# One block of 128 columns for the shared keys and index keys, copied on ScalarE to the rows of their heads

## The chip, the cores and the metric

The kernel runs on one core of one Trainium2 chip. The metric is the device time of the whole program in microseconds (us); a lower time is better. One launch computes everything, and all weights are read from the chip's memory in it.

## The reference, cut to what matters

Two blocks run one after the other on 256 tokens of width 1024: a block of two hybrid attention layers, and a block with a gated delta rule and 16 experts. The change lies in the hybrid layers. Each projects its input with one wide matrix and splits the columns:

```python
h = split_cols(u @ w_in)                     # 4032 columns per layer
dq = rope(h["dsa_q"].reshape(B, S, 4, 64), pos)
dk = rope(h["dsa_k"][:, :, None, :], pos)[:, :, 0]        # 64 columns, one key for 4 heads
iq = rope(h["idx_q"].reshape(B, S, 8, 32), pos)
ik = rope(h["idx_k"][:, :, None, :], pos)[:, :, 0]        # 32 columns, one key for 8 index heads
isc = jnp.einsum("bthd,bsd->bths", iqb, ik)               # scores that choose the top 64 tokens
isc = jnp.einsum("bth,bths->bts", iwb, jax.nn.relu(isc))
...
s = jnp.einsum("bthd,btkd->bthk", qb, kg) * scale         # attention over the chosen tokens
```

The four attention heads share one key of 64 columns, and the eight index heads share one index key of 32.

## The kernel before, in words

Projections are kept transposed: a tile of 128 columns of the projection becomes 128 partitions by 256 tokens. `CHUNKS` lists what is projected in order; most chunks are pairs of such tiles, and one transfer on SyncE's queue brings the 1 MB of weights of a pair into one of two buffers `w`. For each tile `proj_t` calls `halves`, which splits the weights into a rounded part `wh` (a cast on ScalarE, L349) and a remainder `wl` (a subtraction, L350), and then issues 24 matmuls of 128x128 by 256 columns (L438 to L440: eight steps of three).

The heads of a tile stand on different rows (partitions), and a matmul of scores takes query and key from the same rows. So a shared key has to stand on the rows of every head. Before, the columns did that: tile `dk` repeats the 64 key columns twice, and tile `ik` repeats the 32 index key columns four times; both are projected in full. `rope` copies the projected tile to `rraw` on ScalarE (L525), multiplies it by a rotation matrix on TensorE (L531), by the sine on VectorE (L533) and by the cosine on GpSimd (L534), and adds the two on VectorE (L535) into a tile `qk`. `topk` starts when `ik`, `iq0` and `iq1` have been through this.

Which engine subtracts in `halves` is set by a counter over the whole program:

```python
def lo_engine(self):
    self.nsplit += 1
    return self.nc.gpsimd if self.pat[self.nsplit % len(self.pat)] == "P" else self.nc.vector
```

`pat` is "VVP" (every third on GpSimd), except for "P" in chunks 3 to 5 of a layer and a few places of the second block. `act_halves` uses the same counter for activations.

The order of the instructions on each engine is not the order of the code: a scheduler sets it when the program is built, from the dependencies and its own estimate of times, and at run time each engine works through its list in order.

The expert weights (16 experts, 12 transfers of 1 MB each) come through a ring of 21 buffers and the two `w` buffers. They are all issued on SyncE's queue, and a transfer waits until its buffer is free.

Of the kernel before, what the change touches and what calls it, by code (L numbers as in the profile page):

```python
# [34 lines left out]
HALF = slice(0, 64), slice(64, 128)  # L35
# [19 lines left out]
def _cols(name, a, b):  # L55
    return list(range(_OFF[name] + a, _OFF[name] + b))
# [6 lines left out]
    return out  # L63


_TILES = {"dk": _cols("dsa_k", 0, 64) * 2, "ik": _cols("idx_k", 0, 32) * 4}
for _i in range(2):
    _TILES[f"iq{_i}"] = _cols("idx_q", 128 * _i, 128 * _i + 128)
    _TILES[f"dq{_i}"] = _cols("dsa_q", 128 * _i, 128 * _i + 128)
# [8 lines left out]
for _i in range(3):  # L78
# [2 lines left out]
        + _cols("fox_v", 0, 128) + _cols("dsa_v", 0, 32),  # L81
        "NB": _cols("fox_v", 128, 384),
        "NC": _cols("nsa_vs", 0, 128) + _cols("nsa_vw", 0, 128)}
CHUNKS = ["NA", ("dk", "ik"), ("iq0", "iq1"), ("dq0", "dq1"), ("kc", "vc"), ("fq0", "fk0"), "NB",
          ("fq1", "fk1"), ("fq2", "fk2"), "NC", ("ks", "kw"), ("nq0", "nq1"), ("nq2", "g0"), ("g1", "g2"),
          ("g3", "g4"), ("g5", "g6"), ("g7",)]

# [1 line left out]
def _chunk_cols(c):  # L89
    return _NAT[c] if isinstance(c, str) else sum((_TILES[t] for t in c), [])  # L90


WIN_COLS = sum((_chunk_cols(c) for c in CHUNKS), [])
assert sorted(set(WIN_COLS)) == list(range(4032))
WIN_N = len(WIN_COLS)
WIN_OFF = np.cumsum([0] + [len(_chunk_cols(c)) for c in CHUNKS])
MIX_ROWS = list(range(640)) + [640 + 64 * h + i for h in NSA_PERM for i in range(64)]
# [91 lines left out]
def prep(inp):  # L189
# [18 lines left out]
    w = f["w_in"][:, :, WIN_COLS].reshape(2, 8, 128, WIN_N).transpose(0, 2, 1, 3)  # L208
    parts = [w[:, :, :, WIN_OFF[i]:WIN_OFF[i + 1]].reshape(2, 128, -1) for i in range(len(CHUNKS))]
    a["w_in"] = np.concatenate(parts, axis=2)  # L210
# [39 lines left out]
class Kern:  # L250
# [424 lines left out]
    def layer(self, l, uT, x, m, hook, first=None):  # L675

        nc = self.nc
# [3 lines left out]
        S = {}  # L681
        qk = lambda: self.t([128, 256], "qk", 12)
        for i, ch in enumerate(CHUNKS):
            if ch == ("kc", "vc"):
                cc = self.compress_consts(l)
            hook(i)
            self.pat = "P" if 3 <= i < 6 else "VVP"
            w = self.load_chunk(l, i) if l or i else first
            if isinstance(ch, str):
                N = self.t([128, 2, 256], ch)  # L690
                p = self.mmt()
                self.proj_n(p, w, uT)
                nc.vector.tensor_copy(N, p)
                S[ch] = N
                if ch == "NA":
                    self.after_na(N, bf, S)
                continue
            p = self.mmt()
            for ti, name in enumerate(ch):
                q = p[:, ti, :]  # L700
                self.proj_t(q, w[:, :, 128 * ti:128 * ti + 128], uT)
                if name[:2] in ("iq", "ik", "dk", "dq", "ks", "kw"):
                    S[name] = qk()
                    self.rope(S[name], q, 32 if name[0] == "i" else 64)
                elif name in ("kc", "vc"):
                    S[name] = self.compress(cc, 0 if name == "kc" else 1, q)
                elif name[0] == "g":
                    j = int(name[1])
                    e = self.t([128, 256], "ge", 2)
                    self.sigmoid_big(e, q)  # L710
                    nc.vector.tensor_mul(e, e, q)
                    g = S[f"mix{j}"]
                    nc.vector.tensor_mul(g, g, e)
                else:
                    S[name] = qk()
                    nc.scalar.copy(S[name], q)
                    if name[:2] == "nq":
                        S["r" + name] = qk()
                        self.rope_sb(S["r" + name], S[name], 64)
                if name == "iq1":  # L720
                    self.topk(S)
                if name == "dq0":
                    self.dsa(S, 0)
                if name == "dq1":
                    self.dsa(S, 1)
                if name == "vc":
                    self.cmp_finish(cc, S)
                if name[:2] == "fk" and name != "fk1":
                    self.fox(S, int(name[2]))
                if name == "nq2":  # L730
                    self.nsa(S)
            if ch == ("fq1", "fk1"):
                self.fox(S, 1)
# [1252 lines left out]
```

## Time and profile before

| | |
|---|---|
| three runs | 1263.03 us median (1259.28 to 1269.72) |
| profiled execution, own time | 1266.42 us |
| profiled execution, span from first to last instruction | 1264.6 us |
| TensorE busy | 1019.2 us (81% of the span) |
| VectorE / ScalarE / GpSimd busy | 540.9 / 388.1 / 282.4 us |
| data moved | 330 MB, mean 261 GB/s |

The span is 1.8 us shorter than the profiled execution's own time, and that execution was 3.4 us longer than the median. Busy shares are means over stages that differ: the first 820 us hold the two attention layers and the delta rule, the rest the experts.

### The profile page before, as it was taken

Reading aid. Unit: us, or ns where it says so; the run is one execution under the profiler, and the core shown is the slowest. Engines: PE = TensorE matmul, PEld = TensorE weight load, DVE = VectorE, ACT = ScalarE, POOL = GpSimd, SP = SyncE. Lnnn points to the kernel's source line nnn. Section 1 sums busy time; section 2 is a strip of 40 time slices with the busy share of each in tenths; the row PEclk is TensorE's granted clock in tenths of the full one; section 3 lists DMA queues with packets and bytes.
Section 4 is the critical chain, followed back from the end, with each engine's and each line's share of the span. In section 5 each row is a group of like instructions: output and inputs, shape, how many; then the busy total and the mean of one; then the engine's idle time right before and its main releaser. Section 6 shows DMA issues by size and latency. Waiting matters only on the chain. (4 is left out here: it accounts for less than half of the span.)

```text
span 1264.6 us, 22819 instructions
## 1 busy us (share of the span) xinstructions
PE 1019.2 (81%) x9488; PEld 715.0 (57%) x9488; DVE 540.9 (43%) x1269; ACT 388.1 (31%) x905; POOL 282.4 (22%) x253
## 2 busy tenths in 40 slices
PE   5889999978879999948879988897666776676675
PEld 2767777767766777736768777654222332332232
DVE  2585457686687445586585346511000100010002
ACT  2344437636344436535452535210000000000002
POOL 1442132276541231253326352000000000000000
PEclk7899999998799999979989999798888777787678
DMA  9747864334235483621202456799999999999996
GB/s 365 257 161 254 318 236 152 136 128 188 81 105 201 155 316 117 237 98 67 95 24 101 179 231 274 292 382 419 420 421 418 421 418 421 419 420 420 421 419 251
DMA packets 52696, 330.07 MB, mean 261 GB/s; under 512 B 8305, under 2 KB 10097, under 8 KB 14449
## 3 DMA queue, kind: packets, MB, share of 16 engines
q1 hardware_dynamic: 52592, 328.61, 65.9%
q8 instruction: 74, 1.21, 0.4%
q14 instruction: 30, 0.24, 0.0%
HBM read 327.54 MB, written 1.05 MB: 260 GB/s over the span
## 5 line engine op out<-in xcount | busy, mean ns | idle before, releaser
L438 PE MATMUL mm<-uT,wh 128*128 128x256 f32 x576 | 173.3, 301 | 6.4 <-ACT wh L349 3.2
L440 PE MATMUL mm<-uT,wl 128*128 128x256 f32 x576 | 168.4, 293 | 11.2 <-POOL wl L350 9.0
L349 ACT CAST wh<-w 128x1024 fp32r<-128x1024 f32 x124 | 127.9, 1034 | 145.2 <-PE mm L439 81.8
L350 POOL TENSOR_TENSOR wl<-w,wh 128x1024 fp32r<-128x1024 f32 x51 | 123.4, 2423 | 204.5 <-ACT wh L349 186.2
L439 PE MATMUL mm<-uT,wh 128*128 128x256 f32 x576 | 168.5, 293 | 0.0
L440 PEld LDWEIGHTS mm<-uT,wl 128*128 128x128 f32 x576 | 113.1, 197 | 18.0 <-POOL wl L350 10.4
L438 PEld LDWEIGHTS mm<-uT,wh 128*128 128x128 f32 x576 | 113.1, 196 | 17.2 <-issue 7.4
L439 PEld LDWEIGHTS mm<-uT,wh 128*128 128x128 f32 x576 | 113.2, 196 | 6.8 <-issue 6.0
L1847 PE MATMUL o<-rw,XE 128*32 128x256 f32 x944 | 87.4, 475 | 34.7 <-DMA rw<-in_w_gate 34.7
L1847 PE MATMUL g<-rw,XE 128*32 128x256 f32 x928 | 82.7, 462 | 39.4 <-DMA rw<-in_w_up 39.4
L350 DVE TENSOR_TENSOR wl<-w,wh 128x1024 fp32r<-128x1024 f32 x73 | 92.1, 1262 | 51.4 <-ACT wh L349 49.4
L1859 ACT ACTIVATE hd<-o 128x256 f32<-128x256 f32 x16 | 6.1, 384 | 313.0 <-PE o L1847 313.0
L1863 DVE TENSOR_TENSOR hd<-hd,g 128x256 f32<-128x256 f32 x16 | 6.7, 418 | 212.5 <-PE g L1847 212.5
L1891 PE MATMUL mm<-rw,hT 128*32 128x256 f32 x880 | 64.2, 429 | 22.0 <-DMA rw<-in_w_down 16.5
L1847 PEld LDWEIGHTS g<-rw,XE 128*32 128x32 f32 x928 | 31.5, 126 | 84.6 <-DMA rw<-in_w_up 66.0
L1847 PEld LDWEIGHTS o<-rw,XE 128*32 128x32 f32 x944 | 31.8, 129 | 79.5 <-DMA rw<-in_w_gate 54.9
L462 PE MATMUL mm<-wh,uT 128*128 128x256 f32 x256 | 53.8, 298 | 9.7 <-DVE yT L1261 6.6
L1891 PEld LDWEIGHTS mm<-rw,hT 128*32 128x32 f32 x880 | 27.4, 120 | 49.4 <-DMA rw<-in_w_down 22.8
L462 PEld LDWEIGHTS mm<-wh,uT 128*128 128x128 f32 x256 | 41.6, 194 | 15.0 <-ACT wh L349 9.5
L571 ACT ACTIVATE P<-s,nm 128x256 f32<-128x256 f32 (+1 forms) x88 | 35.8, 418 | 28.9 <-DVE nm L564 26.9
L481 PE MATMUL s<-wh,m 128*128 128x512 f32 x128 | 40.9, 396 | 0.0
L462 PE MATMUL mm<-wl,uT 128*128 128x256 f32 x128 | 37.6, 294 | 0.8 <-DVE wl L350 0.7
(645 smaller groups left out, 1941.9 us busy)
## 6 DMA issues: line engine op xcount, KB each, us to landing
rw<-in_w_gate SPq DMA_DIRECT2D x59, 1024.0 KB, 19.9
rw<-in_w_up SPq DMA_DIRECT2D x58, 1024.0 KB, 19.9
rw<-in_w_down SPq DMA_DIRECT2D x55, 1024.0 KB, 19.9
w<-in_w_in SPq DMA_DIRECT2D x48, 1024.0 KB, 4.7
wg<-in_w_mod SPq DMA_DIRECT2D x24, 1024.0 KB, 5.2
wg<-in_w_ada SPq DMA_DIRECT2D x21, 1024.0 KB, 5.5
w<-in_w_out SPq DMA_DIRECT2D x12, 1024.0 KB, 4.8
w<-in_w_up SPq DMA_DIRECT2D x6, 1024.0 KB, 19.8
```

The lines of the kernel that those rows point to most:

```text
L349: self.nc.scalar.copy(hi, w)
L350: self.lo_engine().tensor_sub(lo, w, hi)
L438: mm(out, wh[:, k, :], uh[:, k, :], start=(k == 0), stop=False)
L439: mm(out, wh[:, k, :], ul[:, k, :], start=False, stop=False)
L440: mm(out, wl[:, k, :], uh[:, k, :], start=False, stop=(k == 7))
L462: mm(p[:, tt, :], a[:, k, t], b[:, k % 4, :], start=(k == 0 and tt == 0 and j == 0), stop=(k == 7 and j == 2), skip_group_check=True)
L481: mm(Y(tt, n), a[:, t], b[:, 512 * n:512 * n + 512], start=(k2 == 0 and kk == 0 and i == 0), stop=(k2 == 3 and kk == 1 and i == 2))
L571: nc.scalar.activation(Pm[:, h, o:o + n], S[:, h, o:o + n], AF.Exp, bias=nm[:, i:i + 1], scale=0.125, accum_out=l[:, i:i + 1])
L1847: nc.tensor.matmul(pp[32 * j:32 * j + 32, :], XE[:, k, 32 * (e % 4):32 * (e % 4) + 32], w[:, kk, 256 * j:256 * j + 256], start=(k == 0), s ...
L1859: last = nc.scalar.activation(hd, pg, AF.Silu)
L1863: nc.vector.tensor_mul(hd, hd, pu)
L1891: nc.tensor.matmul(py[32 * j:32 * j + 32, :], hT[:, cb, 32 * jj:32 * jj + 32], w[:, kk, 256 * j:256 * j + 256], start=(k == 0), stop=(k == 7))
```

## The change

`dk` and `ik` become one tile `di` of 128 columns: the 64 key columns and the 32 index key columns twice. It is projected once, as a chunk of its own with 0.5 MB of weights. From the result ScalarE copies rows 0 to 63 to both halves of a tile `rraw` for the keys, and rows 64 to 127 to both halves of another for the index keys. From there `rope_sb` does for each what it did before. The matmuls of scores see the same tiles as before.

```diff
-_TILES = {"dk": _cols("dsa_k", 0, 64) * 2, "ik": _cols("idx_k", 0, 32) * 4}
+_TILES = {"di": _cols("dsa_k", 0, 64) + _cols("idx_k", 0, 32) * 2}
...
-CHUNKS = ["NA", ("dk", "ik"), ("iq0", "iq1"), ("dq0", "dq1"), ("kc", "vc"), ("fq0", "fk0"), "NB",
+CHUNKS = ["NA", ("di",), ("iq0", "iq1"), ("dq0", "dq1"), ("kc", "vc"), ("fq0", "fk0"), "NB",
...
-                if name[:2] in ("iq", "ik", "dk", "dq", "ks", "kw"):
+                if name == "di":
+                    for n, rows, d in (("dk", HALF[0], 64), ("ik", HALF[1], 32)):
+                        raw = self.t([128, 256], "rraw", 2)
+                        for to in HALF:
+                            nc.scalar.copy(raw[to], q[rows])
+                        S[n] = qk()
+                        self.rope_sb(S[n], raw, d)
+                elif name[:2] in ("iq", "dq", "ks", "kw"):
                     S[name] = qk()
                     self.rope(S[name], q, 32 if name[0] == "i" else 64)
```

Per layer there is one call of `halves` less, so the counter of `lo_engine` stands one lower for everything behind it in layer 0, and two lower from layer 1's chunk 2 on. The scheduler builds a new order from this. It shows at three places of layer 0, right behind chunk `NA`. (Lines behind 702 are numbered 8 higher in the changed kernel.)

ScalarE, before: the casts of `dk` and `ik`, then one copy to `rraw` ahead of the cast for `iq0`.

```order
L782 ACTIVATE lfe<-lfe 128x12
L349 CAST wh<-w 128x1024
L783 ACTIVATE lfe<-lfe 128x12
L349 CAST wh<-w 128x1024
L797 CAST foxc<-g 96x256
L663 ACTIVATE c2s<-c2s 128x16
L525 COPY rraw<-mm 128x256
```

ScalarE, changed: the cast of `di` first, and the casts of the next four tiles behind the four copies of `di`.

```order
L349 CAST wh<-w 128x1024
L789 ACTIVATE lfe<-lfx 128x12
L663 ACTIVATE ng<-ng 128x36
L790 ACTIVATE lfe<-lfe 128x12
L791 ACTIVATE lfe<-lfe 128x12
L805 CAST foxc<-g 96x256
L707 COPY rraw<-mm 64x256 x4
L663 ACTIVATE c2s<-c2s 128x16
L349 CAST wh<-w 128x1024 x4
```

What moved: the first cast stands ahead of the activations of `lfe`, and nothing but copies stands between the projection of `di` and the cast that `iq0` needs.

GpSimd, before: the subtraction for `iq0` alone, and two more behind the cosine product of `ik`.

```order
L816 TENSOR_SCALAR foxl<-foxc,c_263 96x256 x2
L534 TENSOR_TENSOR qk<-rraw,c_263 128x256
L816 TENSOR_SCALAR foxl<-foxc,c_263 96x256
L350 TENSOR_TENSOR wl<-w,wh 128x1024
L534 TENSOR_TENSOR qk<-rraw,c_263 128x256
L350 TENSOR_TENSOR wl<-w,wh 128x1024 x2
```

GpSimd, changed: both cosine products of `di`, then three subtractions in a row.

```order
L534 TENSOR_TENSOR qk<-rraw,c_263 128x256
L824 TENSOR_SCALAR foxl<-foxc,c_263 96x256
L534 TENSOR_TENSOR qk<-rraw,c_263 128x256
L824 TENSOR_SCALAR foxl<-foxc,c_263 96x256 x2
L350 TENSOR_TENSOR wl<-w,wh 128x1024 x3
```

What moved: the subtraction for `iq0` went to VectorE, the one for `iq1` came to GpSimd, and no other work parts the three. In layer 1 three subtractions stand in a row as well, where there were two.

VectorE, before, from the copies of `c2v` (a vector of the second block) to its next subtraction, which is that of `iq1`.

```order
L359 COPY c2v<-cc_445 128x256
L533 TENSOR_TENSOR rtmp<-o,c_263 128x256
L359 COPY c2b<-cc_445 128x8x16
L535 TENSOR_TENSOR qk<-qk,rtmp 128x256
L359 COPY c2b<-cc_445 128x8x16
L533 TENSOR_TENSOR rtmp<-o,c_263 128x256
L350 TENSOR_TENSOR wl<-w,wh 128x1024
```

VectorE, changed: the next subtraction is that of `iq0`.

```order
L533 TENSOR_TENSOR rtmp<-o,c_263 128x256
L1117 TENSOR_TENSOR cc_419<-cc_419,c2s 128x16
L535 TENSOR_TENSOR qk<-qk,rtmp 128x256
L359 COPY c2v<-cc_419 128x256
L359 COPY c2b<-cc_419 128x8x16 x2
L350 TENSOR_TENSOR wl<-w,wh 128x1024
```

What moved: both sums of the keys (L535) and the copies now stand ahead of the subtraction on which TensorE's next tile depends. From the second block on, the transfers on SyncE's queue stand in the same order as before.

## Rows read from the trace of the kernel before

**Rows 1.** The page's 40 equal slices: busy tenths of TensorE and of the DMA engines.
```profile
PE   5889999978879999948879988897666776676675
...
DMA  9747864334235483621202456799999999999996
```

**Rows 2.** The chain of waits in order of time: start, us, what.
```profile
734.11 0.12 PE mm L438
...
833.13 16.39 DMA rw<-in_w_up
...
1243.56 10.21 DMA rw<-in_w_down_last
```

**Rows 3.** Timeline, SyncE's queue and TensorE, 800 to 826 us: start, duration, engine, instruction.
```profile
801.62 3.30 SPq L1885 DMA_DIRECT2D w<-in_w_down  x2
...
819.22 0.62 PE L1847 MATMUL o<-rw,XE 128*32 128x256 f32 x2
...
823.20 0.33 SPq L1885 DMA_DIRECT2D rw<-in_w_down  x1
```

**Rows 4.** Windows: length, busy us of PE, PEld, DVE, ACT, POOL; clock, DMA, GB/s.
```profile
43.70:51.30 7.60, 6.80 (x28) 6.06 (x28) 6.27 (x20) 1.60 (x4) 2.49 (x7) 0.55 0.53 169
...
65.00:92.00 27.00, 21.47 (x171) 17.46 (x170) 23.57 (x80) 9.66 (x19) 13.98 (x13) 0.94 0.42 154
...
100.00:262.00 162.00, 157.72 (x1274) 121.21 (x1275) 91.11 (x207) 82.14 (x215) 38.83 (x32) 1.00 0.60 219
```

**Rows 5.** Timeline of layer 0 behind `NA`, 41 to 57 us; in brackets the wait.
```profile
41.27 0.69 DVE L693 COPY NA<-mm 128x512 f32<-128x512 f32 x1 [1.25 <-PE mm L462]
...
42.63 1.03 ACT L349 CAST wh<-w 128x1024 fp32r<-128x1024 f32 x1
...
43.70 1.23 DVE L350 TENSOR_TENSOR wl<-w,wh 128x1024 fp32r<-128x1024 f32 x1 [0.46 <-ACT wh L349]
...
43.72 0.39 PE L438 MATMUL mm<-uT,wh 128*128 128x256 f32 x1 [2.49 <-ACT wh L349]
...
44.98 0.58 PE L440 MATMUL mm<-uT,wl 128*128 128x256 f32 x1 [0.76 <-DVE wl L350]
...
49.20 0.41 PE L438 MATMUL mm<-uT,wh 128*128 128x256 f32 x1
...
49.41 0.41 PE L439 MATMUL mm<-uT,wh 128*128 128x256 f32 x1
...
51.31 0.37 ACT L525 COPY rraw<-mm 128x256 f32<-128x256 f32 x1 [1.09 <-PE mm L440]
...
52.81 2.66 DVE L359 COPY c2b<-cc 128x128 f32<-128x128 f32 x1
53.01 2.39 POOL L350 TENSOR_TENSOR wl<-w,wh 128x1024 fp32r<-128x1024 f32 x1
...
55.73 0.21 DVE L359 COPY c2b<-cc 128x128 f32<-128x128 f32 x1
...
56.07 0.47 PE L440 MATMUL mm<-uT,wl 128*128 128x256 f32 x1
```

**Rows 6.** Groups by line and form on ScalarE, 0 to 110 us: count | busy, mean ns.
```profile
L636 ACT COPY sg<-mm 64x256 f32<-64x256 f32 x4 | 1.5, 366 | 0.0
...
L663 ACT ACTIVATE c2s<-c2s 128x16 f32<-128x16 f32 x1 | 0.2, 216 | 2.5 <-DVE c2s L662 2.5
```

**Rows 7.** Who TensorE waited for until 823 us: total, times, longest.
```profile
PE mm L440 <- POOL wl L350: 11.6, 8, 3.0
```
**Rows 8.** The page's costliest groups: GpSimd's subtractions of the whole span.
```profile
L350 POOL TENSOR_TENSOR wl<-w,wh 128x1024 fp32r<-128x1024 f32 x51 | 123.4, 2423 | 204.5 <-ACT wh L349 186.2
```

**Rows 9.** Timeline of layer 1, chunk 1, 326 to 330 us.
```profile
326.67 4.70 POOL L350 TENSOR_TENSOR wl<-w,wh 128x1024 fp32r<-128x1024 f32 x2
326.74 4.90 DVE L535 TENSOR_TENSOR qk<-qk,rtmp 128x256 f32<-128x256 f32 x1 [0.91 <-POOL qk L534]
...
329.07 0.38 PE L440 MATMUL mm<-uT,wl 128*128 128x256 f32 x1 [1.86 <-POOL wl L350]
```

## The prediction

> **What bounds the kernel now.** I read the page's slices first [rows 1]. They show two halves: TensorE is nearly always busy until about two thirds of the span, and from there the DMA engines are saturated. The chain of waits then shows what the second half hangs on: from 833.13 us to the last block of expert weights it is transfers, one behind the other [rows 2]. The question is when that stream starts. SyncE's queue issues its 23rd expert transfer, which fills the last of the 21 + 2 buffers, by 804.9 us and then stands until 823.20, when TensorE has used up a buffer [rows 3]. TensorE begins with the experts at 819.22, as soon as the tokens are routed. So the DMA engines have nothing to do that they could do earlier, and the remaining 169 of 192 transfers follow at a fixed rate. What the stages ahead of 819 us save or lose reaches the end one to one, as long as the ring fills in time; it was full 14 us ahead.
>
> [...] From 65 to 92 us VectorE, with the search for the top tokens, is busy for 23.57 of 27 us and is as near to being the bound as TensorE with 21.47 [rows 4].
>
> **The change part by part.** *Matmuls.* Each layer loses one projection of 24 matmuls, 48 in all, at 0.12 us from one to the next [rows 2]: -5.8 us if TensorE is the bound there. [...]
>
> *The start of layer 0.* The order on ScalarE puts the cast of `di` ahead of the activations, and VectorE subtracts right after it has copied `NA`. Then the subtraction ends at 41.27 + 0.69 + 1.23 = 43.2 us, where `dk`'s first matmul with the remainder started at 44.98 [rows 5]. That is 1.8 us. At worst it is nothing (weights later than I think), at best both waits, 3.25 us.
>
> *The gap behind `di`.* Here the change takes something back. Before, TensorE had `ik` to do while ScalarE made the copy of `dk` and the cast of `iq0`: from that copy at 51.31 to the undisturbed run of `iq0` at 56.07 are 4.76 us, of which the 24 matmuls of `ik` are 2.9, so 1.9 remain [rows 5]. Now ScalarE has four copies of 64x256 between `di` and that cast. The nearest row is the copy of `sg` in the same shape, 0.366 us [rows 6]: 1.46. Behind them stand the activation of `c2s` with 0.22 [rows 6], the cast with 1.03 and the subtraction on VectorE with 1.23 [rows 5], 3.94 together, and TensorE has only the two rotations to fill it. The price is 3.94 - 1.9 = +2.0. The copies themselves cost ScalarE little: 1.46 against two copies at 0.37 and a cast of 1.03 that are gone. In layer 1 the order lets 7 matmuls of `iq0` run ahead of the first rotation, so its cast is ready there, and I charge nothing; the same 2.0 is the upper bound.
>
> *Who subtracts.* The counter moves, so every later "V" and "P" changes places. I walked the rule through both programs: 51 weight subtractions on GpSimd become 54, and 73 on VectorE become 68. GpSimd's takes 2.42 us [rows 8]. That VectorE has less work is hidden. TensorE waited 11.6 us in all for GpSimd's 51 [rows 7], 0.23 each, so three more are worth +0.7. The bounds are wide, since each lands in another place: from all 11.6 gone to as much again.
>
> *Transfers.* Two of 1 MB become 0.5 MB. They land while TensorE works; at nothing. The search of the top tokens, the ropes' products and sums, and all expert work are the same instructions, and the expert transfers keep their order on SyncE's queue.
>
> The sum is -5.8 - 1.8 + 2.0 + 0.7 = -4.9 us. From the profiled execution's own 1266.4 it gives 1261.5; that execution was 3.4 above the median of the runs shown, so against the median I forecast **1258 us**. A measurement of this kernel can tell about 1% (12.6 us) from no change, its three runs being 10 us apart. The forecast lies inside that.
>
> **The rivals.** *GpSimd holds VectorE up (slower).* While GpSimd's subtraction ran from 53.01 for 2.39 us, VectorE's copy of `c2b` took 2.66; the next one, alone, 0.21 [rows 5]. In layer 1 a sum of a rope took 4.90 us, exactly beside two of GpSimd's subtractions in a row, 4.70 [rows 9]. Now three stand in a row in both layers, and ahead of the subtraction of `iq0` VectorE has two such sums and two such copies. If VectorE isn't through before GpSimd's first one starts (1.03 us after the cast of `iq0`, when the next cast ends), it waits for all three: 3 x 2.42 = 7.3 us in layer 0, in which TensorE has nothing, and the clock falls behind it: 24 x (0.21 - 0.12) = 2.2. In layer 1 the wait grows by one, 2.4. The time is -4.9 + 7.3 + 2.2 + 2.4 = +7.0, or 1270. It decides from two waits on: 4.8 us use up the gain. Against it speaks that VectorE has between 0.9 and 3 us of work there and can be ahead, and that GpSimd waits for casts in its turn, which wait for buffers of `wh`.
>
> [...]
>
> *More falls away (faster).* In layer 1 the rope's sum of 4.90 is that of `ik` in the old place; with both sums of `di` ahead of the subtractions it goes, and with it a wait of TensorE such as the 1.86 at 329.07 [rows 9]. If the like happens in layer 0 (3.25 instead of 1.8 at its start) and TensorE's waits for GpSimd shrink by a third (3.9) instead of growing by 0.7, the sum is -4.9 - 1.9 - 1.4 - 4.6 = -12.8, or 1250.
>
> *Nothing arrives.* If from 65 to 92 us VectorE sets the end of the search, and the ends of the layers hang on VectorE, the matmuls saved are waited for instead; then -1 or so from the earlier start remains: 1262. For it speaks the 23.57 of 27 [rows 4], against it the 157.72 of 162 behind.
>
> *Another order.* The scheduler has reordered both layers, beyond the places that I could price. This has no sign; I take up to 15 us either way.
>
> **How the numbers follow.** The forecast, between 1255 and 1261: 0.40. Nothing arrives, 1261 to 1265: 0.20. GpSimd holds VectorE up, 1265 to 1277: 0.17. More falls away, 1246 to 1255: 0.13. Another order: 0.05 beyond 1272 and 0.05 below 1248. The range is **1246 to 1270**: at its low end it takes in all of the faster rival, and at the high end the slower one up to its worked-out price; what is left out is 0.04 below and about 0.10 above. Faster by over 1%, below 1250.4: 0.05 of other orders, half of the faster rival and a rest of the forecast's own error, 0.15. Slower by over 1%, above 1275.7: 0.05 and a fourth of the slower rival, 0.10. Within 1%: 0.75.
>
> **What the profile of the changed kernel would show.** TensorE's matmuls fall by 48: from 576 to 560 in each of the groups L438 to L440, eight per line and layer. The first matmul of `di` with the remainder stands near 43.2 us, and between `di` and `iq0` TensorE waits about 2.5 us for a cast. ScalarE's copies of 64x256 take 0.37 each. `iq0` runs some 2 to 3 us earlier than at 56.07. If the slower rival is right, VectorE's sums or subtraction there are 2.4 to 7 us long instead of 0.4 to 1.2, and `iq0` starts behind 58. The first expert matmul would be near 814, 5 us ahead of 819.22, and the transfers behind it keep their rate. I would be wrong if the ring weren't full when the routing ends, or if a wait in a stage that I didn't look at (the ends of the layers, the second block) grew by more than the sum.

## The result, and the profile after

The changed kernel takes 1270.95 us (median of 20 runs, 1268.02 to 1274.93), against 1264.53 us (20 runs) for the kernel before: a ratio of 1.0059, with a 95% interval of 1.0044 to 1.0075. It is slower by 0.6%: 6.4 us between the two medians, some 7.5 by the ratio, where 4.9 us faster had been forecast. The profiled execution has a span of 1272.6 us and took 1274.40 us in all, 8.0 us more than that of before and 3.4 more than the median of the changed kernel.

First the groups of one of TensorE's three projection lines and of the subtractions on GpSimd and VectorE, from the page of the changed kernel (busy us, mean ns | idle before):

```profile
L440 PE MATMUL mm<-uT,wl 128*128 128x256 f32 x560 | 164.4, 294 | 16.8 <-DVE wl L350 11.1
...
L350 POOL TENSOR_TENSOR wl<-w,wh 128x1024 fp32r<-128x1024 f32 (+1 forms) x54 | 127.9, 2373 | 192.4 <-ACT wh L349 171.7
...
L350 DVE TENSOR_TENSOR wl<-w,wh 128x1024 fp32r<-128x1024 f32 (+1 forms) x68 | 84.6, 1246 | 42.2 <-ACT wh L349 39.8
```

TensorE has the 48 matmuls less that were meant to go: 560 instead of 576 in each of L438 to L440, and its busy time on the page falls from 1019.2 to 1012.9 us. The work is gone, and the time isn't. GpSimd has 54 subtractions instead of 51 [rows 8], VectorE 68, as counted.

The end of the program answers to [rows 2, 3]. This is SyncE's queue and TensorE's first expert matmul in the changed kernel (start, duration), and one row of the chain of waits:

```profile
811.98 3.29 SPq L1893 DMA_DIRECT2D w<-in_w_down  x2
830.91 0.33 SPq L1893 DMA_DIRECT2D rw<-in_w_down  x1
```
```profile
826.93 0.62 PE L1855 MATMUL o<-rw,XE 128*32 128x256 f32 x2
```
```profile
834.36 12.75 DMA rw<-in_w_up
...
1251.29 10.24 DMA rw<-in_w_down_last
```

The ring is full by 815.3 us, 11.7 us ahead of the first expert matmul at 826.93, and SyncE stands until 830.91. The first expert matmul is 7.71 us later than at 819.22, the last block's transfer 7.73 later than at 1243.56. So the loss is made ahead of the experts and passes through one to one; the question is where ahead of 827 us.

Layer 0 behind `NA` answers to [rows 5]. These are ScalarE's, VectorE's, GpSimd's and TensorE's timelines there (start, duration; in brackets the wait):

```profile
46.88 1.51 ACT L707 COPY rraw<-mm 64x256 f32<-64x256 f32 x4 [0.90 <-PE mm L440]
...
48.54 2.92 ACT L349 CAST wh<-w 128x1024 fp32r<-128x1024 f32 x3
```
```profile
51.17 5.24 DVE L1117 TENSOR_TENSOR cc<-cc,c2s 128x16 f32<-128x16 f32 x1
...
57.14 1.21 DVE L350 TENSOR_TENSOR wl<-w,wh 128x1024 fp32r<-128x1024 f32 x1
```
```profile
50.43 1.35 POOL L824 TENSOR_SCALAR foxl<-foxc,c 96x256 bf16<-96x256 bf16 x2
51.75 4.63 POOL L350 TENSOR_TENSOR wl<-w,wh 128x1024 fp32r<-128x1024 f32 x2
```
```profile
43.37 0.39 PE L440 MATMUL mm<-uT,wl 128*128 128x256 f32 x1 [1.68 <-DVE wl L350]
...
47.68 0.70 PE L531 MATMUL o<-rraw,c 128*128 128x256 f32 x2 [0.83 <-ACT rraw L707]
50.01 0.67 PE L531 MATMUL o<-rraw,c 128*128 128x256 f32 x2 [1.63 <-DVE rtmp L533]
...
58.41 0.58 PE L440 MATMUL mm<-uT,wl 128*128 128x256 f32 x1 [7.49 <-DVE wl L350]
58.78 0.41 PE L438 MATMUL mm<-uT,wh 128*128 128x256 f32 x1
59.00 0.41 PE L439 MATMUL mm<-uT,wh 128*128 128x256 f32 x1
...
61.77 0.28 PE L440 MATMUL mm<-uT,wl 128*128 128x256 f32 x1
61.89 0.28 PE L438 MATMUL mm<-uT,wh 128*128 128x256 f32 x1
```

Read them from the bottom. TensorE's first matmul of `iq0` with the remainder runs at 58.41, after 7.49 us of waiting for VectorE's subtraction. That takes its usual 1.21 us, from 57.14; its cast was made long before (three casts from 48.54 to 51.46). What VectorE did from 51.17 to 56.41 is a product of 128x16 elements. The same product took 0.18 us at 50.93 in the kernel before and 0.16 at 49.39 in iq_dq_on_vector, both times beside scalings of GpSimd but no subtraction. This one began beside a scaling of GpSimd, which two subtractions follow without a gap (`iq1`'s and `dq0`'s), and it ends when these do, at 56.38. Only two stood in a row here: GpSimd's third subtraction of the list came 7.41 us later, behind its cast. Behind the wait matmuls stand 0.21 us apart until 61.56 and 0.12 apart from 61.77; the granted clock was 0.50 from 58.40 to 61.60 and 0.95 from 61.60 to 63.00.

In layer 1 the same happens at another step, ahead of the search. VectorE, GpSimd and TensorE there:

```profile
335.86 7.88 DVE L535 TENSOR_TENSOR qk<-qk,rtmp 128x256 f32<-128x256 f32 x1
```
```profile
335.10 0.73 POOL L534 TENSOR_TENSOR qk<-rraw,c 128x256 f32<-128x256 f32 x1
335.79 6.99 POOL L350 TENSOR_TENSOR wl<-w,wh 128x1024 fp32r<-128x1024 f32 x3
342.74 0.72 POOL L534 TENSOR_TENSOR qk<-rraw,c 128x256 f32<-128x256 f32 x1
```
```profile
343.79 1.23 PE L841 MATMUL s<-qk 32*128 32x256 f32 x6 [5.70 <-DVE qk L535]
```

A sum of the rope, 0.42 us at 322.41 in the kernel before with nothing of GpSimd's beside it, takes 7.88: it ends just behind three subtractions of GpSimd (`dq0`, `dq1`, `kc`) and a product that follows them without a gap. TensorE waits 5.70 us for it, where in the kernel before it waited 1.86 for a subtraction [rows 9] and 1.21 at this place:

```profile
338.13 1.24 PE L833 MATMUL s<-qk 32*128 32x256 f32 x8 [1.21 <-DVE qk L535]
```

The list of TensorE's waits until its first expert work, which answers to [rows 7], has these (total, times, longest):

```profile
PE mm L440 <- DVE wl L350: 11.7, 5, 7.5
...
PE mm L440 <- POOL wl L350: 8.3, 4, 3.6
...
PE s L841 <- DVE qk L535: 5.7, 1, 5.7
```

The second of these stood in the kernel before as [rows 7], and the first as:

```profile
PE mm L440 <- DVE wl L350: 2.3, 3, 0.8
```

The waits for GpSimd fell from 11.6 to 8.3 us, and those for VectorE's remainders rose from 2.3 to 11.7. Counted on GpSimd's account alone, as the forecast did, the new turns look like a gain.

To see where time is lost along the program, the start of the same VectorE instruction is compared in every profile. In us, the kernel before and then the difference to it; the last column is what the second block adds, from its start to the routing:

```
                       search 0  layer 0 end  search 1  block 2  routed  block 2 adds
kernel before             68.23       266.35    340.03   565.62  814.52
changed                   +3.14        +2.88    +10.49    +4.12   +8.97     +4.9
turns_kept                -0.67        -2.01     -3.58    -7.86   -6.26     +1.6
turns_moved               +1.83        +1.68     +6.02    -4.61   +0.25     +4.9
iq_on_vector              +1.18        -0.08     +4.98    -2.08   +1.81     +3.9
iq_dq_on_vector           -3.14        -1.75     -4.02    -7.45   -1.19     +6.3
after_block2              +3.06        +2.67    +10.36    +2.60   +3.92     +1.3
before_block2             -0.58        -1.17     -0.67    +0.57   +7.89     +7.3
vector_block2             -1.14        +2.93     +2.05    -2.59   +0.28     +2.9
di_twice                  -1.28        -1.31     -1.98    -6.28   -9.09     -2.8
ik_short                  +0.61        -0.20     +1.29    -3.74   -0.20     +3.5
one_to_gpsimd             -0.68        -0.90     -1.35    -0.80   -0.75     +0.1
one_to_vector             +1.88        +2.96     +9.14    +3.30   +3.99     +0.7
kept_iq_dq_vector         -3.09        +0.34     -6.25    -9.51   -8.66     +0.9
```

Each is one execution, and some lie well off the median of their kernel's runs: that of turns_moved 4.4 us under it, those of before_block2 and vector_block2 3.5 and 9.1 us over it. Kernels that are the same up to block 2 show how far two executions differ: the changed one, after_block2 and one_to_vector by 1.5 us or less, the kernel before, before_block2 and one_to_gpsimd by 1.4 or less, but iq_dq_on_vector and vector_block2 by up to 6.1. So the table hints at where, and the times below say how much. The changed kernel loses 3 us to the first search, comes into the second block 4.1 us late, and loses 4.9 more in the block, which computes nothing that was changed.

### The profile page after: what moved, and what is told of

Same layout as the page of the kernel before. It is cut to its first block, busy times and chain, and to the rows that moved or that the text cites. A ratio compares the mean times of both kernels' runs of the same rounds, so it can differ in the third digit from the quotient of the medians.

```text
span 1272.6 us, 22745 instructions
## 1 busy us (share of the span) xinstructions
PE 1012.9 (80%) x9440; PEld 710.6 (56%) x9440; DVE 538.9 (42%) x1266; ACT 390.4 (31%) x907; POOL 278.9 (22%) x254
## 3 DMA queue, kind: packets, MB, share of 16 engines
q8 instruction: 74, 1.21, 0.4%
## 4 chain that ended last, share of the span: by engine, by line
PE 39%; DMA 36%; DVE 12%; ACT 5%; POOL 5%; issue 3%; POOLq 0%; SPq 0%; DVEq 0%; ACTq 0%
DMA rw<-in_w_up 14%; DMA rw<-in_w_down 11%; DMA rw<-in_w_gate 5%; PE mm L438 4%; PE mm L440 4%; PE mm L439 4%; PE s L481 3%; DMA w<-in_w_up 3%; PE g L377 3%; PE mm L462 3%; DMA wg<-in_w_ada 2%; POOL wl L350 2%; ACT wh L349 2%; PE o L588 2%; PE s L559 1%
## 5 line engine op out<-in xcount | busy, mean ns | idle before, releaser
L440 PE MATMUL mm<-uT,wl 128*128 128x256 f32 x560 | 164.4, 294 | 16.8 <-DVE wl L350 11.1
L349 ACT CAST wh<-w 128x1024 fp32r<-128x1024 f32 (+1 forms) x122 | 125.6, 1033 | 149.3 <-PE mm L439 91.7
L438 PE MATMUL mm<-uT,wh 128*128 128x256 f32 x560 | 167.9, 300 | 4.3 <-DVE yT L1269 2.0
L350 POOL TENSOR_TENSOR wl<-w,wh 128x1024 fp32r<-128x1024 f32 (+1 forms) x54 | 127.9, 2373 | 192.4 <-ACT wh L349 171.7
L439 PE MATMUL mm<-uT,wh 128*128 128x256 f32 x560 | 164.8, 295 | 0.0
L440 PEld LDWEIGHTS mm<-uT,wl 128*128 128x128 f32 x560 | 110.1, 197 | 23.8 <-DVE wl L350 12.1
L438 PEld LDWEIGHTS mm<-uT,wh 128*128 128x128 f32 x560 | 110.4, 197 | 13.9 <-issue 6.8
L439 PEld LDWEIGHTS mm<-uT,wh 128*128 128x128 f32 x560 | 110.3, 197 | 7.4 <-issue 6.6
L1855 PE MATMUL o<-rw,XE 128*32 128x256 f32 x944 | 83.5, 455 | 34.8 <-DMA rw<-in_w_gate 34.8
L350 DVE TENSOR_TENSOR wl<-w,wh 128x1024 fp32r<-128x1024 f32 (+1 forms) x68 | 84.6, 1246 | 42.2 <-ACT wh L349 39.8
L1899 PE MATMUL mm<-rw,hT 128*32 128x256 f32 x880 | 60.4, 405 | 24.8 <-DMA rw<-in_w_down 19.2
```

Source lines behind the costliest of these rows:

```text
L349: self.nc.scalar.copy(hi, w)
L350: self.lo_engine().tensor_sub(lo, w, hi)
L438: mm(out, wh[:, k, :], uh[:, k, :], start=(k == 0), stop=False)
L439: mm(out, wh[:, k, :], ul[:, k, :], start=False, stop=False)
L440: mm(out, wl[:, k, :], uh[:, k, :], start=False, stop=(k == 7))
L1855: nc.tensor.matmul(pp[32 * j:32 * j + 32, :], XE[:, k, 32 * (e % 4):32 * (e % 4) + 32], w[:, kk, 256 * j:256 * j + 256], start=(k == 0), s ...
```

## The experiments

Three theories stood at first: HOLD, that VectorE is held up by GpSimd right ahead of what TensorE waits for; TURNS, that the new places of all subtractions cost a little each; and ORDER, that the order of instructions behind the first chunk, which differs nearly everywhere, is what costs. All ratios are to the kernel before, with 95% intervals, from 12 runs each (6 for one_to_vector) against 29 to 35 of the kernel before measured beside them. Where orders of instructions are compared, the numbers are those outside the longest sequence that both traces share, until the tokens are routed.

**turns_kept.** The changed kernel, and the counter goes on by one more at `di`:

```diff
                 if name == "di":
-
+                    self.nsplit += 1
                     for n, rows, d in (("dk", HALF[0], 64), ("ik", HALF[1], 32)):
```

> The changed kernel, with the counter moved on by one more behind di, so that every later subtraction is on the same engine as in the kernel before (iq0 of layer 0 on GpSimd, iq1 on VectorE). Theory HOLD (VectorE is held up by GpSimd's subtractions right ahead of the step that TensorE waits for: iq0's remainder in layer 0, 7.49 us; the rope's sum before the search in layer 1, 5.70 us): iq0's remainder of layer 0 is made by GpSimd from about 51.8 to 54.2 us, TensorE's wait falls from 7.49 to about 3.3 us, layer 1 stays as it is, and the time is 1263 to 1267. Theory TURNS (the new places of all subtractions are what costs, in both layers and the second block): as forecast without the turns, 1258 to 1260. Theory ORDER (the instructions behind the first chunk stand in another order on every engine, and that costs, whoever subtracts): 1269 to 1273, and the second block loses again.

1260.29 us, 0.9979 (0.9956 to 1.0001). With the subtractions where they were, the change is 0.8% (some 10 us) better than without, and no longer slower than the kernel before. This run alone doesn't set ORDER aside: its order differs from that of the kernel before in 94 of some 1,140 instructions of VectorE and 409 of some 5,900 of TensorE, the changed kernel's in 190 and 685, so the order came back halfway with the turns. The time lies just above TURNS' range (1258 to 1260) and below HOLD's (1263 to 1267). In layer 0 it goes as HOLD said:

```profile
50.05 6.43 DVE L664 TENSOR_SCALAR c2s<-c2s 128x16 f32<-128x16 f32 x1
```
```profile
47.98 0.73 POOL L534 TENSOR_TENSOR qk<-rraw,c 128x256 f32<-128x256 f32 x1 [1.81 <-ACT rraw L707]
49.41 0.62 POOL L824 TENSOR_SCALAR foxl<-foxc,c 96x256 bf16<-96x256 bf16 x1 [0.70 <-DVE foxc L812]
50.00 0.73 POOL L534 TENSOR_TENSOR qk<-rraw,c 128x256 f32<-128x256 f32 x1
50.71 1.09 POOL L824 TENSOR_SCALAR foxl<-foxc,c 96x256 bf16<-96x256 bf16 x2
51.77 4.67 POOL L350 TENSOR_TENSOR wl<-w,wh 128x1024 fp32r<-128x1024 f32 x2
```
```profile
54.16 0.58 PE L440 MATMUL mm<-uT,wl 128*128 128x256 f32 x1 [2.98 <-POOL wl L350]
```

TensorE waits 2.98 us instead of 7.49. VectorE is held up for even longer (6.43 us for 128x16 elements), but nobody waits for it there: `iq0`'s remainder is GpSimd's own first subtraction. In layer 1 the hold stays, with 5.96 us of waiting ahead of the search (see below, ik_short, for its rows in another kernel).

**turns_moved.** The kernel before, with the counter not moved on by `ik`:

```diff
-                self.proj_t(q, w[:, :, 128 * ti:128 * ti + 128], uT)
+                self.proj_t(q, w[:, :, 128 * ti:128 * ti + 128], uT); self.nsplit -= name == "ik"
```

> The kernel before, with both projections of dk and ik, but ik's subtraction doesn't move the counter on, so that from iq0 on every subtraction is on the engine that it has in the changed kernel. HOLD: while TensorE still has ik to do, VectorE is free for iq0's remainder before GpSimd starts, so nothing is held up there; within 3 us of the kernel before, 1262 to 1268. TURNS: the whole loss without the saving, 4.9 + 6.4 = 11 us more than before, near 1275. ORDER: the order changes behind the first chunk as much as by the real change, so a few us either way, with no sign.

1269.88 us, 1.0039 (1.0011 to 1.0067). The turns alone, without any change of the projections, make the kernel before slower by 0.4%. That is above what HOLD allowed and half of what TURNS asked for. Another order comes with them, though (175 of VectorE's instructions and 576 of TensorE's stand elsewhere). Where the median loses its time the profile can't tell, since the profiled execution took 1265.51 us and is no slower than that of the kernel before. In it the kernel is 4.6 us ahead at block 2 and loses 4.9 in the block, for which HOLD had no term.

**iq_on_vector.** The changed kernel, `iq1`'s subtraction on VectorE too:

```diff
-            self.pat = "P" if 3 <= i < 6 else "VVP"
+            self.pat = "V" if i == 2 else "P" if 3 <= i < 6 else "VVP"
```

> The changed kernel, but iq1's subtraction is on VectorE too (iq0's is already), in both layers; the counter runs as before and the order of instructions is the changed kernel's but for about 40 matmuls. HOLD: in layer 0 one of GpSimd's two subtractions that held up VectorE (5.24 us for an operation of 0.2) is gone, so the hold-up is about 2.4 to 2.9, TensorE's wait for iq0's remainder 5.1 instead of 7.49, and the time 2 to 3 us under the changed kernel, 1268 to 1269; layer 1's 5.70 stays, since dq0, dq1 and kc hold VectorE up there. TURNS: one subtraction less on GpSimd in each layer, about 0.5. ORDER: no difference, 1271.

1267.94 us, 1.0024 (1.0003 to 1.0046); the changed kernel has 1.0059. Layer 0 is as forecast to the tenth: one subtraction of GpSimd is left, VectorE's next instruction is held for 2.80 us, and TensorE waits 5.04.

```profile
51.52 2.80 DVE L359 COPY c2v<-cc 128x256 f32<-128x256 f32 x1
```
```profile
51.84 2.33 POOL L350 TENSOR_TENSOR wl<-w,wh 128x1024 fp32r<-128x1024 f32 x1
```
```profile
55.78 0.58 PE L440 MATMUL mm<-uT,wl 128*128 128x256 f32 x1 [5.04 <-DVE wl L350]
```

Layer 1's sum is still held (7.20 us, 5.56 of waiting). The order is nearly the changed kernel's (3 of VectorE's and 7 of TensorE's instructions stand elsewhere), so the gain of 0.35%, 4.4 us, can hardly come from that. It is more than the 2 to 3 us expected, but its interval is some 3.4 us wide to either side. This is the cleanest test of HOLD here, and it covers layer 0 alone.

**iq_dq_on_vector.** As the last, with `if i in (2, 3)`: `dq0` and `dq1` too.

> The changed kernel, but the subtractions of iq1, dq0 and dq1 are on VectorE too, in both layers, so that GpSimd subtracts nothing until kc. HOLD: VectorE's operation of 5.24 us in layer 0 and its sum of 7.88 us in layer 1 fall to 0.2 to 0.5 us, TensorE's waits of 7.49 and 5.70 to about 2.5 and 2, of which VectorE's three more subtractions of 1.25 give back up to 2.5 in each layer ahead of the search: 1260 to 1266. TURNS: three subtractions less on GpSimd in each layer at 0.23: 1269 to 1270. ORDER: no sign, since a third of the order changes; the holds may go, but the time needn't follow.

1261.54 us, 0.9981 (0.9957 to 1.0005): 0.8% better than the changed kernel, within HOLD's range. With no subtraction of GpSimd beside them, the sums and the small products are short again (0.42 us for the sum at 49.57, 0.16 for the product below); TensorE's waits are 2.72 us for `iq0`'s remainder and 1.26 ahead of layer 1's search:

```profile
49.39 0.16 DVE L1117 TENSOR_TENSOR cc<-cc,c2s 128x16 f32<-128x16 f32 x1
```
```profile
51.86 0.58 PE L440 MATMUL mm<-uT,wl 128*128 128x256 f32 x1 [2.72 <-DVE wl L350]
```
```profile
334.63 0.71 PE L841 MATMUL s<-qk 32*128 32x256 f32 x8 [1.26 <-DVE qk L535]
```

VectorE has three more subtractions in each layer and the time falls: it was not its load that counted, but, by the waits, what stood beside it. Another order comes with this edit too (81 of VectorE's and 282 of TensorE's instructions), so it is the waits, and iq_on_vector, that speak for HOLD, more than the time alone. How much of the time is layer 1's hold and how much the order isn't shown.

**after_block2** and **before_block2.** The counter moved for the second block alone, so that its subtractions there are where the other kernel has them; the first is the changed kernel, the second the kernel before:

```diff
-        R = {"pre": "l"}
+        R = {"pre": "l"}; self.nsplit += 2
```
```diff
-        R = {"pre": "l"}
+        R = {"pre": "l"}; self.nsplit -= 2
```

> The changed kernel, with the counter moved on by two at the start of the second block, so that there, and only there, every subtraction is on the same engine as in the kernel before. The stages up to 565 us are the changed kernel's, instruction for instruction. Theory TURNS2 (the second block's loss, from 4.1 us at its start to 9.0 us at the routing, is the price of who subtracts there): it keeps the 4.1 us and loses nothing more, 1265 to 1267. Theory ORDER2 (it is the order that the scheduler finds when the block starts late and from another state): 1270 to 1272.

> The kernel before, with the counter two less from the start of the second block, so that its subtractions there are on the engines that they have in the changed kernel; everything up to 565 us is the kernel before. TURNS2: the block loses 4 to 6 us, 1268 to 1271. ORDER2: within 1.5 us of the kernel before, 1263 to 1266.

1269.09 us, 1.0037 (1.0018 to 1.0057), and 1269.44 us, 1.0035 (1.0014 to 1.0055). The second fulfils TURNS2: 0.35%, 4.4 us, for other turns in block 2 and the order that the scheduler builds from them (up to the block both orders are the same; in it 35 of VectorE's 291 instructions and 121 of TensorE's 2,120 stand elsewhere). The first gains 0.2% only, inside the intervals, and lies between the two theories. **vector_block2** is iq_dq_on_vector with `self.nsplit += 2` there:

> The changed kernel with iq1's, dq0's and dq1's subtractions on VectorE in both layers (1261.5 us so far) and the second block's turns as in the kernel before. HOLD and TURNS2 together: the 7.5 us that it is ahead of the kernel before at 565 us are kept to the end, 1256 to 1258, the best of all. ORDER2: 1260 to 1263.

1257.42 us, 0.9951 (0.9923 to 0.9980), 0.3% better than iq_dq_on_vector, again inside the intervals. Over the three pairs the second block's turns, with their order, cost 0.22, 0.35 and 0.30%, 3.7 us on average; the average is clear of the noise (some 1.6 to 5.8 us), of the pairs the middle one alone. In the table the five kernels with the changed kernel's turns add 3.9 to 7.3 us in the block, and the six with those of the kernel before -2.8 to 3.5.

In the profiles the block's loss isn't in what TensorE stands idle but in the clock. From the block's start to the routing it is idle for 32.4 of 248.9 us in the kernel before and 33.5 of 256.2 in before_block2; it is busy for 216.5 and 222.8 us, at a granted clock of 0.92 and 0.89. This is the stretch from 600 to 625 us in the windows of the kernel before and of before_block2 (length; busy us of PE, PEld, DVE, ACT, POOL; granted clock), and two of before_block2's matmul rows:

```profile
600.00:625.00 25.00, 22.31 (x271) 19.44 (x269) 14.15 (x34) 10.19 (x34) 4.04 (x4) 1.00 0.24 85
```
```profile
600.00:625.00 25.00, 20.01 (x262) 17.23 (x259) 11.59 (x26) 5.59 (x21) 4.31 (x3) 0.80 0.24 84
```
```profile
605.40 0.39 PE L440 MATMUL mm<-uT,wl 128*128 128x256 f32 x1 [1.44 <-POOL wl L350]
...
611.15 0.41 PE L439 MATMUL mm<-uT,wh 128*128 128x256 f32 x1
611.36 0.41 PE L440 MATMUL mm<-uT,wl 128*128 128x256 f32 x1
```

TensorE waits 1.44 us for a subtraction that is now GpSimd's, and its matmuls behind stand 0.21 us apart, where in the kernel before they are 0.12 apart at a granted clock of 1.00. It is the same in every profile: from 600 to 625 us the five kernels with the changed kernel's turns in the block have a granted clock of 0.80 to 0.86, the other nine 1.00.

**one_to_gpsimd** and **one_to_vector** move that one subtraction alone, the 115th of the kernel before and the 113th of the changed one:

```diff
-        return self.nc.gpsimd if self.pat[self.nsplit % len(self.pat)] == "P" else self.nc.vector
+        return self.nc.gpsimd if self.pat[self.nsplit % len(self.pat)] == "P" or self.nsplit == 115 else self.nc.vector
```

> The kernel before, with a single weight subtraction moved from VectorE to GpSimd: that of the third tile of v's columns in the second block (at 607.2 us in the kernel before), and the order nearly untouched. Theory CLOCK2 (the second block's 4 to 6 us are the price of one wait of TensorE for this subtraction, behind which the granted clock is at the lower level until about 618 us): TensorE's wait at 608.5 grows from 0.76 to 1.4 to 2 us, the clock granted from 600 to 625 us falls from 1.00 to about 0.8, and the time is 4 to 6 us up, 1268 to 1271. Theory SUM2 (the loss is the sum of many small moves): about 1 us up, 1265 to 1266.

> The changed kernel with that one subtraction back on VectorE, nothing else moved. CLOCK2: the granted clock behind it is 1.00 again and the time 4 to 6 us down, 1265 to 1267. SUM2: 1270.

1265.48 us, 1.0018 (1.0001 to 1.0036), and 1269.04 us, 1.0049 (1.0033 to 1.0065). CLOCK2 isn't borne out as it stood. In the first the wait didn't come: 0.78 us at 608.56, and the clock stayed at 1.00. In the second the clock from 600 to 625 us is back at 1.00 and the block adds 0.7 us instead of 4.9 in the profile, but the times gain no more than 0.1%, inside the intervals. So in the changed kernel that one subtraction sets the clock of this stretch, but hardly the time. That the turns of block 2, with the order built from them, cost some 4 us is shown; which of its 41 subtractions it is, and whether it is the turns or the order, is open.

**di_twice.** turns_kept, with `di`'s 24 matmuls made twice:

```diff
-        for k in range(8):
+        for k in list(range(8)) * rep:
```
(`rep` is 2 for `di` and 1 for all others.)

> The kernel with the turns kept, but TensorE makes the projection of di twice over (24 matmuls more in each layer, into the same place of PSUM, the second pass starting anew), so that it has all the matmuls of the kernel before and still one cast and one subtraction less in each layer. If the matmuls saved were worth the forecast's 48 x 0.12 = 5.8 us: 1265 to 1267. If what is worth something is the missing cast and subtraction: within 2 us of the 1260.3 of the kernel with the turns kept.

1257.27 us, 0.9959 (0.9937 to 0.9981), with as many matmuls as the kernel before. The 48 matmuls cost nothing that can be measured; the time is 0.2% under that of turns_kept, inside the intervals, and 1 us lower than the second expectation allowed. **ik_short** asks the same from the other side: the kernel before, and `ik` from one of eight row blocks.

```diff
-                self.proj_t(q, w[:, :, 128 * ti:128 * ti + 128], uT)
+                self.proj_t(q, w[:, :, 128 * ti:128 * ti + 128], uT, 1 if name == "ik" else 8)
```

> The kernel before, but ik is projected from the first of its eight row blocks alone: 21 of its 24 matmuls are left out in each layer (42 in all), so that ik's values are wrong, while casts, subtractions, turns, copies and ropes are all there. If matmuls left out at this place are worth 0.12 us each: 42 x 0.12 = 5.0, 1259 to 1260. If TensorE only comes earlier to the same wait (as the projection made twice says): 1263 to 1266.

1264.76 us, 1.0016 (1.0002 to 1.0029), with 42 matmuls fewer and no gain. The profile of its layer 1 tells what becomes of them, on VectorE, GpSimd and TensorE:

```profile
327.32 7.85 DVE L535 TENSOR_TENSOR qk<-qk,rtmp 128x256 f32<-128x256 f32 x1 [1.22 <-POOL qk L534]
```
```profile
327.26 4.66 POOL L350 TENSOR_TENSOR wl<-w,wh 128x1024 fp32r<-128x1024 f32 x2
331.88 0.71 POOL L534 TENSOR_TENSOR qk<-rraw,c 128x256 f32<-128x256 f32 x1
332.56 2.33 POOL L350 TENSOR_TENSOR wl<-w,wh 128x1024 fp32r<-128x1024 f32 x1
```
```profile
335.23 1.22 PE L833 MATMUL s<-qk 32*128 32x256 f32 x4 [6.77 <-DVE qk L535]
```

In the kernel before, the rope's sum was free again after two of GpSimd's subtractions [rows 9], and the third came only at 334.57. Here TensorE is through sooner, the third subtraction follows at once, and the sum is held until 335.2 us. TensorE waits 6.77 us ahead of the search, which starts 1.3 us later in this execution than with all matmuls.

There is a second reason why the number of matmuls doesn't show, and no run here tells it from the first: the granted clock goes with them. From 317 to 345 us it is 0.70 in turns_kept and 0.80 with `di` made twice, 0.81 in the kernel before and 0.69 in ik_short; from 41 to 75 us it is 0.90 and 0.95, 0.90 and 0.85. Where TensorE had less to do, the mean granted clock was lower in these stretches. Both kernels also have another order than the one they are compared with (116 and 84 of VectorE's instructions).

**kept_iq_dq_vector.** turns_kept with the subtractions of `iq` and `dq` on VectorE.

> The turns kept, and iq0's, iq1's, dq0's and dq1's subtractions on VectorE in both layers, so that GpSimd holds VectorE up in neither: the sum of HOLD's two parts. HOLD: layer 0 as with the turns kept, layer 1's 5.96 us of wait ahead of the search fall to about 1.5, 1255 to 1258, as the best so far (1257.4). If VectorE is now the bound ahead of the search: 1260.

1258.81 us, 0.9959 (0.9942 to 0.9977). That is just above HOLD's range, though the holds are gone as expected: TensorE waits 2.73 us for `iq0`'s remainder and 1.20 ahead of layer 1's search. It can't be told from vector_block2 and di_twice; the three are the fastest, 0.4 to 0.5% under the kernel before.

## Why the prediction was wrong

*What bounds the kernel* was right: the ring was full ahead of the routing, and 7.7 us at the first expert matmul are 7.7 at the last block's transfer.

*Matmuls, -5.8 us: the step that failed first.* They were counted at full price, 0.12 us each, which holds if TensorE is the bound where they stand. From 100 to 262 us it nearly is, busy for 157.72 of 162 us [rows 4], but the matmuls don't stand there. They lie in front of the search, where TensorE waits for what ScalarE, VectorE and GpSimd make. Making them twice cost nothing (-0.2% against turns_kept), and leaving 42 of them out of the kernel before gave nothing (+0.16%), the granted clock falling or rising with their number (from 317 to 345 us, 0.70 and 0.80 with `di` made twice, 0.81 and 0.69 with 42 left out). The rival that nothing arrives had this with a chance of 0.20, though it looked for the reason on VectorE in the search itself, 65 to 92 us.

*The start of layer 0, -1.8*, was right: the first matmul with the remainder at 43.37 instead of 44.98, 1.6 us. Its upper bound of 3.25 is the sum of the waits at 43.72 and 44.98, 2.49 and 0.76 [rows 5].

*The gap behind `di`, +2.0*, was too small even without a hold. ScalarE's four copies took 1.51 us and the casts came as forecast. But the sum went through ScalarE's queue alone and left out what VectorE and GpSimd have to do before they subtract. In iq_dq_on_vector, where VectorE subtracts and nothing holds it, TensorE's three waits between `di` and `iq0` are 0.83 + 1.63 + 2.72 = 5.2 us. In turns_kept GpSimd's two products for the rope and its scalings of `foxc` go on until 51.80, and only then its subtraction starts, 1.9 us behind the end of the cast (48.82 + 1.03). The three waits are 0.83 + 1.63 + 2.98 = 5.4 us there, and 0.83 + 1.63 + 7.49 = 10.0 in the changed kernel; about 2.5 had been forecast.

*Who subtracts, +0.7: the step that failed most.* It is 0.8%, some 10 us, by turns_kept against the changed kernel, the orders built from the turns included. The price was taken as the mean of what TensorE waited for GpSimd, 0.23 us for one. The number of GpSimd's subtractions isn't what costs; one that stands beside a step of VectorE which TensorE waits for can cost its whole length (iq_on_vector takes one away, and the wait falls from 7.49 to 5.04), and behind the longer wait the granted clock was 0.50 from 58.40 to 61.60 us.

*The rival "GpSimd holds VectorE up"*, with a chance of 0.17, is what the rows show in both layers, and its price of 1270 us is 1 us from the time. It named the places, and the kind of instruction that is held. In layer 1 its size was right too: 2.4 us more, where 5.70 took the place of 1.86 + 1.21, 2.6 more. In layer 0 its 7.3 us for three subtractions next to the measured wait of 7.49 is chance: VectorE's product took 5.24 beside a scaling and two subtractions, the rest of the wait is VectorE's own work behind, and without a hold 2.72 us of it remain. As to who comes first: had VectorE's product of 51.17 taken the 0.16 us that it takes in iq_dq_on_vector, with 1.04 us of work behind it (0.41 + 0.28 + 0.35), the subtraction would have begun at 52.4 instead of 57.14, if GpSimd's first subtraction, at 51.75, hadn't held the rest. GpSimd's scaling began 0.7 us earlier than the product and its subtraction 0.6 later, so which came first was a matter of under a microsecond, and no row that the prediction shows could have told it. Nor does any run show whether the one that comes first holds the other up. What the trace shows is that VectorE's product took 5.24 us, where 0.16 was its time in iq_dq_on_vector, over the ends of a scaling and of a first subtraction.

That the rival's sum is right is largely luck. It counted 7.3 + 2.2 + 2.4 = 11.9 us for the holds; without the 3.7 us of the second block, turns cost 10 - 3.7 = 6.3. Its 2.2 for the clock takes all 24 matmuls of a tile at 0.21 us apart, as at 49.20 and 49.41 [rows 5], instead of 0.12; behind the wait of 7.49 us only 15 ran slower, the 3.36 us from 58.41 to 61.77, an estimated 1.6 us more than 15 x 0.12. A part of what is lost at a hold seems to be made up behind it (10.5 us at layer 1's search are 4.1 at block 2 in the profile of the changed kernel); how, no run shows. It didn't know of the second block's 3.7. And it took 5.6 us for the rest of the change (-5.8 - 1.8 + 2.0), where with turns kept 2.7 were measured (0.21%).

*Open.* Why the change is better than the kernel before when turns are kept (0.2%, its interval just touching 1) and more so with the matmuls made twice: the start of layer 0, one cast and one subtraction less in each layer, another order and another granted clock all go together, and no run took them apart. How much of the 10 us is the holds and how much the orders that came with the turns: 4.4 us, with iq_on_vector, are the one part in which the order hardly moved. And the single step in the second block, as said above.

## What to carry to other kernels

A saving on the busiest engine is worth something only where that engine sets the pace: look at the next wait behind the place before pricing it. A counter that hands out work in turns makes every removal a change of all that follows, so pin the engine of each step by name before taking one out, or put the count back. And when one engine's steps can stretch another's, as GpSimd's subtractions did with VectorE's here (5.24 us for a product of 0.16), look at what stands beside a step in time, and not only at how many there are.

## What the runs showed of the hardware

A held VectorE can stay held over several instructions of GpSimd that follow without a gap: in turns_kept 6.43 us passed for one instruction of 128x16 elements, over a product, two scalings and two subtractions from 50.00 to 56.44, and in layer 1 of the changed kernel 7.88 us over four. But it isn't always so. In the kernel before, a sum of the rope that began beside the first of two such subtractions ended at 60.53, while the second ran on until 62.78:

```profile
57.93 2.60 DVE L535 TENSOR_TENSOR qk<-qk,rtmp 128x256 f32<-128x256 f32 x1
```
```profile
57.64 5.14 POOL L350 TENSOR_TENSOR wl<-w,wh 128x1024 fp32r<-128x1024 f32 x2 [1.10 <-DMA wg<-in_w_ada]
```

These two subtractions took 5.14 us, where two took 4.63 to 4.70 in the rows above. The sum of [rows 9], too, ended at 331.64, behind two subtractions but beside a product that began at 331.32. What decides whether VectorE gets in between, no run shows.

Not all of VectorE's instructions are held. One that reads PSUM ran at its usual length within a subtraction of GpSimd, in the changed kernel (0.42 us, the mean of its eight):

```profile
674.24 2.37 POOL L350 TENSOR_TENSOR wl<-w,wh 128x1024 fp32r<-128x1024 f32 x1 [10.04 <-ACT wh L349]
```
```profile
674.98 0.42 DVE L1584 TENSOR_TENSOR X<-E,s 128x256 f32<-128x256 f32 x1 [0.44 <-PE s L1338]
```

Four other steps of VectorE with an operand in PSUM that fell within GpSimd's subtractions there took 0.42 us as well (at 443.21, 460.28, 485.17 and 701.02), while an instruction with one input in SBUF, that of 128x12 elements at 324.56 (L794), took 2.33 us beside a subtraction, where it took 0.17 at 43.79. That isn't true of every one: a reciprocal of 128x16 elements in SBUF took 0.24 us at 50.73, as at 48.95 in iq_dq_on_vector, beside GpSimd's scalings from 50.43 to 51.78.
